# Input norm of a hybrid decoder layer: the refined reciprocal root kept in PSUM, its square taken by ScalarE

## The chip, the cores and the metric

One Trainium2 chip, one of its cores. The metric is the device time of one execution in microseconds; the kernel before has a median of 1319.98 us over 3 runs (1318.55 to 1320.32). The engines are named as the profile names them: PE (TensorE matmul), PEld (its weight loads), DVE (VectorE), ACT (ScalarE), POOL (GpSimd), SP (SyncE, which issues the DMAs).

## The reference

One layer over 1024 tokens of width 1024, all in float32. What matters here is the first step, an RMS norm whose result `u` feeds one wide projection; the two head groups, the output projection, a gated per-layer embedding and a final norm follow.

```python
def rmsnorm(x, w):
    xf = x.astype(jnp.float32)
    y = xf * lax.rsqrt(jnp.mean(xf * xf, axis=-1, keepdims=True) + NORM_EPS)
    return (y * w.astype(jnp.float32)).astype(x.dtype)

def reference(x, p, norm_w, w_in, ...):
    u = rmsnorm(h, norm_w[i])
    proj = jnp.einsum('bsd,de->bse', u, w_in[i])
    hq, hf, hi, hg, fq, fk, fv, fg, fz = jnp.split(proj, SPLIT_POINTS, axis=-1)
    y_h = hgrn2_branch(hq, hf, hi, lb_all[i], hgrn_gn[i]) * jax.nn.silu(hg)
    y_f = fox_branch(fq, fk, fv, fz, fox_fb[i]) * jax.nn.silu(fg)
    h = h + jnp.einsum('bse,ed->bsd', jnp.concatenate([y_h, y_f], axis=-1), w_out[i])
    ple = jnp.einsum('bsk,kd->bsd', p[i], w_ple[i])
    h = h + jax.nn.sigmoid(jnp.einsum('bsd,de->bse', h, w_ple_gate[i])) * ple
    return rmsnorm(h, final_norm_w)
```

## The kernel before

**Layout.** Activations lie transposed: 8 tiles of 128 channels (index k) by 1024 tokens. Tokens are worked in two halves of 512 (index c). Every float32 product is made of three matmuls on halves of a split: each operand is written as hi + lo, where hi is the value rounded by ACT to the matmul's input format (L82) and lo the rest, a subtraction on POOL or DVE (L83). L98, L99 and L100 are the three matmuls of a term.

**The opening, up to about 68 us.** x is loaded and squared (ACT), the squares of the 8 tiles are added up (DVE, `acc`), and one matmul with a matrix of ones (L253, L257) leaves in a PSUM bank `ssq[c]` the sum of squares of each token, the same in all 128 partitions. `rstd` (L119 to L122) makes the reciprocal root of it: ACT's table function gives y, and DVE refines it by one Newton step, y (1.5 - 0.5 s y y) with s the mean square. Then `u_norm` (L275) multiplies each of the 8 tiles of x by norm_w (a per-partition scalar) and by the root, in place, on DVE, and `u_split` makes uhi (ACT) and ulo (DVE for k = 0, 3, 7, POOL for the other five). Half 0 goes first, then half 1.

PE meanwhile makes `pple`, 16 pieces of p times w_ple, which ACT or DVE halves into `pleo` and SP stores for the end, and then `token_major`, the first 8 blocks of values v: blocks 0 to 3 need u of half 0, blocks 4 to 7 u of half 1, each of them 24 matmuls over all 8 tiles k. DVE copies each block out of PSUM (L149). POOL also makes the lo parts of the first weights (`wtlo`, then `wlo`).

**Order.** What is passed through `pin` keeps the order of the program on its engine; each engine runs its instructions in that order and waits at one for what it needs. So a DVE instruction that is late makes all DVE instructions behind it late. The matmuls of `token_major` are not pinned and are placed between the pinned ones by the scheduler.

**After the opening** come dense projections (L364), among which the recurrent heads and then the attention heads are worked in pieces, the output projection, the gate and the final norm. The final norm calls `rstd` too (L1094 on), which stays as it is.

**PSUM.** `pple` has 4 banks, `ssq` 2, and the products `ps` 2.

Of the kernel before, what the change touches and what calls it, by code (L numbers as in the profile page):

```python
# [12 lines left out]
AF = mybir.ActivationFunctionType  # L13
ALU = mybir.AluOpType
# [5 lines left out]
D = 1024  # L20
# [44 lines left out]
def trunk(ctx: ExitStack, tc: tile.TileContext, a, out):  # L65
    nc = tc.nc
# [18 lines left out]
    def load_w(src, k, lo_engine=None, pin=lambda ins: ins):  # L85

        wf = wpool.tile([P, KT, P], F32, name="wf", tag="wf", bufs=2)
        nc.sync.dma_start(out=wf[:, :k], in_=src)
        hi = wpool.tile([P, KT, P], F32R, name="whi", tag="whi")
        lo = wpool.tile([P, KT, P], F32R, name="wlo", tag="wlo")  # L90
        split(hi[:, :k], lo[:, :k], wf[:, :k], lo_engine or nc.gpsimd, pin)
        return hi, lo
# [24 lines left out]
    def rstd(y, t, ps, pin=lambda ins: ins):  # L117

        pin(nc.scalar.activation(y, ps, AF.Abs_reciprocal_sqrt, scale=1.0 / D))  # L119
        pin(nc.vector.tensor_tensor(out=t, in0=y, in1=y, op=ALU.mult))  # L120
        pin(nc.vector.scalar_tensor_tensor(out=t, in0=ps, scalar=-0.5 / D, in1=t, op0=ALU.mult, op1=ALU.mult))
        pin(nc.vector.scalar_tensor_tensor(out=y, in0=t, scalar=1.5, in1=y, op0=ALU.add, op1=ALU.mult))  # L122

    def operands(*names):

        return [[tuple(upool.tile([P, CH], F32R, name=name, tag="u") for name in names) for _ in range(KT)] for _ in range(NCH)]


    wt_st = ExitStack()
# [13 lines left out]
    def token_major(w, v, blocks, evac_pin=lambda ins: ins):  # L143

        for b in blocks:
            ps = pp.tile([P, 2 * P], F32, name="ps", tag="proj")
            sl = slice(b % 4 * P, (b % 4 + 1) * P)
            product(ps, [(u[b // 4][j][0][:, sl], u[b // 4][j][1][:, sl], w[0][:, j], w[1][:, j]) for j in range(KT)])
            evac_pin(nc.vector.tensor_copy(out=v[:, :, b], in_=ps.rearrange("p (i d) -> p i d", i=2)))  # L149

    with ExitStack() as st:
# [3 lines left out]
        pin = tc.keep_in_program_order  # L155

        vecs = const.tile([P, 4, KT], F32, name="vecs")
        norm_w, gn_w, lb_log, fin_w = (vecs[:, i, :] for i in range(4))
# [36 lines left out]
        def ple(*pieces):  # L195
            for i in pieces:
                n, c = i % KT, i // KT
                _, hi, lo = wple[n // 4]
                pple[i] = sps.tile([P, CH], F32, name="pple", bufs=4)
                product(  # L200
                    pple[i], [(hi[:, n % 4, j], lo[:, n % 4, j], phi[:, j, half[c]], plo[:, j, half[c]]) for j in range(2)], pin
                )

        def ple_out(i, act):
            n, c = i % KT, i // KT
            o = sp2.tile([P, CH], F32, name="pleo", bufs=7)
            if act:
                pin(nc.scalar.activation(o, pple[i], AF.Copy, scale=0.5))
            else:
                pin(nc.vector.tensor_scalar(out=o, in0=pple[i], scalar1=0.5, scalar2=None, op0=ALU.mult))  # L210
            nc.sync.dma_start(out=pled[n, :, half[c]], in_=o)
# [40 lines left out]
        ssq = [sps.tile([P, CH], F32, name="ssq") for _ in range(NCH)]  # L252
# [6 lines left out]
        first_pair = [wt.tile([P, KT, 2 * P], F32R, name=name) for name in ("wthi", "wtlo")]  # L259
        rs, newt = ([sp2.tile([P, CH], F32, name=name) for _ in range(NCH)] for name in ("rstd", "newt"))  # L260
        u = operands("uhi", "ulo")
        cst = const.tile([P, P + 32], F32, name="cst")
        nc.sync.dma_start(out=cst, in_=a["consts"])
# [4 lines left out]
        def split_pair(i):  # L268
            sl = slice(i * P, (i + 1) * P)
            split(first_pair[0][:, :, sl], first_pair[1][:, :, sl], wf_v[i], nc.gpsimd, pin)  # L270

        def u_norm(k, c):
            x = xs[k][:, half[c]]
            pin(
                nc.vector.scalar_tensor_tensor(  # L275
                    out=x, in0=x, scalar=norm_w[:, k : k + 1], in1=rs[c], op0=ALU.mult, op1=ALU.mult
                )
            )

        def u_split(k, c, lo_engine):  # L280
            split(*u[c][k], xs[k][:, half[c]], lo_engine, pin)

        v = v0p.tile([P, 2, FB, P], F32, name="v", tag="v")
        split_pair(0)
        rstd(rs[0], newt[0], ssq[0], pin)
        split_pair(1)
        ple_out(7, True)
        ple(11)
        for c in range(NCH):
            for k in range(KT):  # L290
                u_norm(k, c)
                if k:
                    u_split(k - 1, c, nc.vector if k - 1 in (0, 3, 7) else nc.gpsimd)
                if c and k in (0, 1, 4, 6):
                    b = (0, 1, 4, 6).index(k)
                    token_major(first_pair, v, range(b, b + 1), pin)
                if c == 0 and k in (2, 4, 6, 7):
                    i = 8 + (2, 4, 6, 7).index(k)
                    ple_out(i, True)
                    ple(i + 4)  # L300
            u_split(7, c, nc.vector)
            if c == 0:
                rstd(rs[1], newt[1], ssq[1], pin)
                for i in range(12, 16):
                    ple_out(i, True)
            else:
                first_f = load_w(a["w_in"][T_HF], KT, nc.gpsimd, pin)
                token_major(first_pair, v, range(FB // 2, FB))
# [192 lines left out]
    with ExitStack() as st:  # L501
# [8 lines left out]
        for i in range(2):  # L510
            t = hs.tile([P, FB, P], F32, name=f"st{i}")
            nc.gpsimd.memset(t, 0.0)
            st_t.append(t)
            t = hs.tile([P, FB, 32], F32, name=f"r{i}")
# [256 lines left out]
    with fox as st:  # L771
# [181 lines left out]
        for n, ch in enumerate(chunks):  # L953
            p, i, c = ch.p, ch.i, ch.c
# [33 lines left out]

        first_w = ahead.weights()
        y_h = operands("yhi", "ylo")  # L990
        for c in range(NCH):
            sl = slice(c * CH, (c + 1) * CH)
# [4 lines left out]
    with ExitStack() as st:  # L997
# [34 lines left out]
        with tc.tile_pool(name="yp", bufs=2 * KT, reuse_waits="tile") as yp:  # L1032

            y_f = [[] for _ in range(NCH)]
            w = [first_w, load_w(a["w_out"][1], KT, nc.vector, tc.keep_in_program_order)]
            for n in range(KT):
                dense(None, y_h, ev_h1(n), w=w[n])
                w.append(load_w(a["w_out"][n + 2], KT, nc.vector, tc.keep_in_program_order))
                hi, lo = (yp.tile([P, S], F32R, name=name, tag="y") for name in ("yhi", "ylo"))
                y = g01.tile([P, S], F32, name="yf", tag="g")  # L1040
                nc.sync.dma_start(out=y, in_=yd[KT + n])
                split(hi, lo, y, nc.vector, tc.keep_in_program_order)
                for c in range(NCH):
                    y_f[c].append(tuple(t[:, c * CH : (c + 1) * CH] for t in (hi, lo)))
            for n in range(2):
                gw[n] = load_gate(n, g01, ("ghi", "glo"), tag="g")

            hm = operands("hh", "hl")
            for n in range(KT):
                dense(a["w_out"][KT + n], y_f, ev_h(n), lo_engine=nc.vector, w=w[KT + n] if n < 2 else None)  # L1050
# [109 lines left out]
```

## Time and profile before

| | |
|---|---|
| median of 3 runs | 1319.98 us (1318.55 to 1320.32) |
| the profiled execution | 1317.97 us |
| its span, first to last instruction | 1316.2 us |
| mean granted PE clock | 0.994 |
| busy: PE, DVE, ACT, POOL | 1270.2, 799.8, 475.0, 351.2 us |
| first dense product (L364) | at 68.11 us |

A row of the timeline reads: start in us, duration in us, engine, line, operation, output <- inputs, shape, count; in brackets the idle time of the engine before it and what ended that. A row with x2 or x3 stands for so many instructions in a line, and its duration runs from the first start to the last end. The duration of an instruction holds whatever it waits for once it has been started. A group row gives the shortest, the median and the longest duration in ns, or the busy time and the mean. A windows row gives, for a stretch, each engine's busy time with the number of instructions, the granted clock, the DMA share and GB/s.

### The profile page before, as it was taken

The page shows a single profiled execution, that of the slowest core. Times are in us where ns is not written, and L with a number is a line of the kernel's source. Part 1 is how long each engine was busy: PE and PEld are TensorE (multiplying, and loading weights), DVE is VectorE, ACT ScalarE, POOL GpSimd, SP SyncE. Part 2 cuts the span into 40 slices and gives each one's busy share as a digit, 9 for nine tenths or more (in the row PEclk, how much of TensorE's full clock was granted, in tenths as well). Part 3 has the DMA queues.
Part 4 walks back from the last instruction along what each step waited for, and adds up shares of the span by engine and source line. Part 5 has one row for each costly group of instructions (what it writes and reads, how often), then busy time and mean ns, then how long its engine had stood idle before and what let it go on. Part 6 is the DMA issues. An engine that isn't in the chain of part 4 may idle for free.

```text
span 1316.2 us, 26795 instructions
## 1 busy us (share of the span) xinstructions
PE 1270.2 (97%) x10996; PEld 1014.5 (77%) x10996; DVE 799.8 (61%) x1988; ACT 475.0 (36%) x1144; POOL 351.2 (27%) x288
## 2 busy tenths in 40 slices
PE   6899999999999999999999999999999999999996
PEld 4787888889788877776777777776666788888895
DVE  6746565745657486377666666667788733333465
ACT  5523121312313124254444444444554411212454
POOL 3613122111212122324342434332322200102232
PEclk9999999999999999999999999999999999999998
DMA  7312102111111020211221212121232653212321
GB/s 290 131 48 65 50 18 80 49 34 48 50 49 33 33 64 22 81 58 57 90 72 59 74 58 74 57 74 57 81 101 79 211 194 99 80 48 74 118 79 66
DMA packets 38970, 102.22 MB, mean 78 GB/s; under 512 B 6720, under 2 KB 8896, under 8 KB 38848
## 3 DMA queue, kind: packets, MB, share of 16 engines
q1 hardware_dynamic: 38704, 99.99, 22.9%
q8 instruction: 86, 1.41, 0.4%
q0 software_dynamic: 144, 0.52, 0.1%
q14 instruction: 36, 0.29, 0.1%
HBM read 83.07 MB, written 17.43 MB: 76 GB/s over the span
## 4 chain that ended last, share of the span: by engine, by line
PE 80%; DVE 9%; ACT 6%; issue 2%; DMA 1%; POOL 1%; SPq 0%; DVEq 0%; ACTq 0%; POOLq 0%
PE ps L364 46%; PE lg L816 5%; PE ps L100 4%; PE po L864 4%; PE ps L98 4%; PE ps L99 4%; ACT x L852 2%; PE ps L571 1%; PE gps L100 1%; PE gps L99 1%; PE gps L98 1%; DVE x L275 1%; PE po L712 1%; PE po L714 1%; DVE x L830 1%
## 5 line engine op out<-in xcount | busy, mean ns | idle before, releaser
L364 PE MATMUL ps<-uhi,whi 128*128 128x512 f32 x896 | 360.1, 402 | 0.0
L364 PE MATMUL ps<-ulo,whi 128*128 128x512 f32 x896 | 354.4, 396 | 0.0
L364 PE MATMUL ps<-uhi,wlo 128*128 128x512 f32 x896 | 352.5, 393 | 0.0
L83 POOL TENSOR_TENSOR wlo<-wf,whi 128x1024 fp32r<-128x1024 f32 x59 | 144.9, 2456 | 453.4 <-ACT whi L82 424.1
L364 PEld LDWEIGHTS ps<-uhi,whi 128*128 128x128 f32 x896 | 168.2, 188 | 58.5 <-issue 21.6
L364 PEld LDWEIGHTS ps<-uhi,wlo 128*128 128x128 f32 x896 | 168.4, 188 | 35.6 <-issue 1.1
L364 PEld LDWEIGHTS ps<-ulo,whi 128*128 128x128 f32 x896 | 168.4, 188 | 33.6 <-issue 0.7
L852 ACT ACTIVATE x<-x,mxo 128x512 f32<-128x512 f32 (+15 forms) x256 | 130.4, 511 | 68.4 <-DVE mxo L840 68.4
L82 ACT CAST whi<-wf 128x1024 fp32r<-128x1024 f32 (+1 forms) x77 | 79.7, 1036 | 204.2 <-PE ps L99 89.8
L830 DVE CUSTOM_DVE_ANT_0 x<-lg,fb 128x512 f32<-128x512 f32 (+15 forms) x256 | 101.8, 434 | 78.4 <-PE lg L816 71.5
L853 DVE STREAM_TRANSPOSE pt<-x 128x512 f32<-128x512 f32 (+15 forms) x256 | 115.1, 457 | 37.9 <-ACT x L852 33.9
L98 PE MATMUL ps<-yhi,whi 128*128 128x512 f32 x256 | 99.8, 390 | 1.7 <-DVE h L1012 1.7
L99 PE MATMUL ps<-ylo,whi 128*128 128x512 f32 x256 | 99.7, 390 | 0.3 <-DVE ylo L83 0.3
L100 PE MATMUL ps<-yhi,wlo 128*128 128x512 f32 x256 | 99.6, 389 | 0.0
L816 PE MATMUL lg<-k,q 64*32 64x480 f32 (+15 forms) x1024 | 74.4, 396 | 2.6 <-DVE mx L830 2.6
L816 PE MATMUL lg<-k,qx 64*32 64x512 f32 (+15 forms) x1024 | 74.4, 396 | 0.0
L864 PEld LDWEIGHTS po<-pt,v 64*64 64x64 f32 x1536 | 53.6, 133 | 22.7 <-issue 9.2
L864 PE MATMUL po<-pt,v 64*64 64x256 f32 (+7 forms) x1536 | 69.4, 320 | 0.0
L98 PEld LDWEIGHTS ps<-yhi,whi 128*128 128x128 f32 x256 | 48.0, 188 | 12.2 <-ACT whi L82 2.1
L99 PEld LDWEIGHTS ps<-ylo,whi 128*128 128x128 f32 x256 | 48.1, 188 | 10.7 <-DVE ylo L83 0.8
L100 PEld LDWEIGHTS ps<-yhi,wlo 128*128 128x128 f32 x256 | 48.0, 188 | 9.8
L364 PE MATMUL ps<-wthi,uhi 128*128 128x256 f32 x192 | 54.0, 281 | 0.0
(205 smaller groups left out, 2158.0 us busy)
## 6 DMA issues: line engine op xcount, KB each, us to landing
wf<-in_w_in_dram SPq DMA_DIRECT2D x64, 512.0 KB, 3.5
fb<-fd SPq DMA_DIRECT2D x64, 128.0 KB, 3.2
yf<-yd SPq DMA_DIRECT2D x16, 512.0 KB, 5.9
wf<-in_w_out_dram SPq DMA_DIRECT2D x16, 512.0 KB, 3.6
x<-in_xT_dram SPq DMA_DIRECT2D x8, 512.0 KB, 9.4
pled<-pleo SPq DMA_DIRECT2D x16, 256.0 KB, 3.3
yd<-sg SPq DMA_DIRECT2D x8, 512.0 KB, 2.6
rz<-zd SPq DMA_DIRECT2D x16, 256.0 KB, 3.4
```

Of the source, the lines that this page charges most:

```text
L82: pin(nc.scalar.copy(hi, src))
L83: pin(lo_engine.tensor_tensor(out=lo, in0=src, in1=hi, op=ALU.subtract))
L98: pin(mm(ps, whi, uhi, start=i == 0, stop=False))
L99: pin(mm(ps, whi, ulo, start=False, stop=False))
L100: pin(mm(ps, wlo, uhi, start=False, stop=i == n - 1))
L275: nc.vector.scalar_tensor_tensor(out=x, in0=x, scalar=norm_w[:, k : k + 1], in1=rs[c], op0=ALU.mult, op1=ALU.mult)
L364: pe(mm(ps, x, y, start=i == j == 0, stop=i == n - 1 and j == 2))
L816: mm(ps[32 * j : 32 * j + 32, m % 2, : 32 * n], q[:, 32 * (j // 2) :][:, :32], k[not own][rows].rearrange("p (t a k) -> p t a k", a=2, k=3 ...
L830: nc.vector.tensor_tensor_reduce(out=x, in0=ps[:, m % 2, : 32 * n], in1=copies[m % 2][:, : 32 * n], scale=1.0, scalar=BIG, op0=ALU.add, op ...
L852: nc.scalar.activation(x, x, AF.Exp, bias=self.other[:, g : g + 1], scale=-1.0, accum_out=zs[:, m : m + 1])
L853: nc.vector.transpose(self.probs[:, : m + 1, g], x.rearrange("p (t k) -> p t k", k=32))
L864: mm(po[half[t % 2], r, 32 * first : 256], v_t[self.p][half[r], t ^ r, half[self.i]], self.probs[half[r], t, first:].rearrange("p g q -> p ...
```

## The change

A new helper `rstd_in_place` stands in for `rstd` at the two calls of the input norm. ACT makes the first estimate y as before (now L130) and also its square (L131, into the tile `newt`). DVE then makes the Newton step in two instructions that write into the bank of `ssq` itself: L132 replaces s by -0.5 s y y, L133 that by (1.5 + it) y. `u_norm` (now L282) takes its factor from `ssq[c]` in PSUM and no longer from the SBUF tile `rs[c]`. The same numbers are multiplied in the same order; the square is made by another engine.

```diff
+    def rstd_in_place(y, t, ps, pin):
+        pin(nc.scalar.activation(y, ps, AF.Abs_reciprocal_sqrt, scale=1.0 / D))
+        pin(nc.scalar.activation(t, y, AF.Square))
+        pin(nc.vector.scalar_tensor_tensor(out=ps, in0=ps, scalar=-0.5 / D, in1=t, op0=ALU.mult, op1=ALU.mult))
+        pin(nc.vector.scalar_tensor_tensor(out=ps, in0=ps, scalar=1.5, in1=y, op0=ALU.add, op1=ALU.mult))
...
@@ u_norm
-                    out=x, in0=x, scalar=norm_w[:, k : k + 1], in1=rs[c], op0=ALU.mult, op1=ALU.mult
+                    out=x, in0=x, scalar=norm_w[:, k : k + 1], in1=ssq[c], op0=ALU.mult, op1=ALU.mult
...
-        rstd(rs[0], newt[0], ssq[0], pin)
+        rstd_in_place(rs[0], newt[0], ssq[0], pin)
...
-                rstd(rs[1], newt[1], ssq[1], pin)
+                rstd_in_place(rs[1], newt[1], ssq[1], pin)
```

All lines behind the helper are 7 higher in the changed kernel (L275 is L282, L149 is L156). On DVE, at the start of half 0, the order of instructions changes thus (`x_92` and `x_93` are the tiles of x for k = 0 and 1):

```order
 L115 TENSOR_TENSOR acc<-acc,sq 128x512 x2
-L120 TENSOR_TENSOR newt<-rstd 128x512
-L121 SCALAR_TENSOR_TENSOR newt<-ssq,newt 128x512
-L122 SCALAR_TENSOR_TENSOR rstd<-newt,rstd 128x512
-L275 SCALAR_TENSOR_TENSOR x_92<-x_92,vecs,rstd 128x512
-L275 SCALAR_TENSOR_TENSOR x_93<-x_93,vecs,rstd 128x512
+L132 SCALAR_TENSOR_TENSOR ssq<-ssq,newt 128x512
+L133 SCALAR_TENSOR_TENSOR ssq<-ssq,rstd 128x512
+L282 SCALAR_TENSOR_TENSOR x_92<-x_92,vecs,ssq 128x512
+L282 SCALAR_TENSOR_TENSOR x_93<-x_93,vecs,ssq 128x512
 L83 TENSOR_TENSOR ulo<-x_92,uhi 128x512
```

One instruction of three is gone, and the factor of the norm is read from `ssq`. The same holds at the start of half 1; behind it DVE's order is unchanged. On ACT, at the same place:

```order
 L82 CAST wthi<-wf 128x8x128
-L119 ACTIVATE rstd<-ssq 128x512
+L130 ACTIVATE rstd<-ssq 128x512
+L131 ACTIVATE newt<-rstd 128x512
 L82 CAST wthi<-wf 128x8x128
```

The square stands right behind the root, ahead of the second cast of the first weights. On PE three matmuls of `token_major` stand some places earlier, and POOL and SP have the same instructions in the same order.

## The prediction

> **What bounds the kernel now.** I read the share of the chain first, then three stretches of the span, then the rows of each engine between 25 and 60 us, where the changed lines run.
>
> ```profile
> PE 80%; DVE 9%; ACT 6%; issue 2%; DMA 1%; POOL 1%; SPq 0%; DVEq 0%; ACTq 0%; POOLq 0%
> ...
> 30.00:68.11 38.11, 32.06 (x220) 28.64 (x219) 29.37 (x33) 17.55 (x28) 24.43 (x17) 0.96 0.36 119
> 68.11:100.00 31.89, 31.89 (x143) 26.42 (x142) 14.51 (x28) 6.71 (x10) 4.78 (x2) 1.00 0.12 42
> 100.00:1316.20 1216.20, 1185.31 (x10565) 944.40 (x10563) 736.85 (x1910) 431.46 (x1081) 312.20 (x261) 0.99 0.22 71
> ...
> 68.11 0.39 PE L364 MATMUL ps<-uhi,whi 128*128 128x512 f32 x1
> ```
>
> The columns after the width are the busy time of PE, PEld, DVE, ACT and POOL, then the granted clock. From the first dense product at 68.11 us on, PE is busy 31.89 of 31.89 us and then 97%: what moves that start moves the end. Before it, PE is not the limit; DVE is, and half of its time there is waiting:
>
> ```profile
> 26.44 2.47 DVE L120 TENSOR_TENSOR newt<-rstd 128x512 f32<-128x512 f32 x1 [1.25 <-ACT rstd L119]
> 28.94 0.69 DVE L121 SCALAR_TENSOR_TENSOR newt<-ssq,newt 128x512 f32<-128x512 f32 x1
> 29.67 2.07 DVE L122 SCALAR_TENSOR_TENSOR rstd<-newt,rstd 128x512 f32<-128x512 f32 x1
> 31.78 1.42 DVE L275 SCALAR_TENSOR_TENSOR x<-x,vecs,rstd 128x512 f32<-128x512 f32 x2
> 33.21 0.69 DVE L83 TENSOR_TENSOR ulo<-x,uhi 128x512 fp32r<-128x512 f32 x1
> 33.82 4.12 DVE L275 SCALAR_TENSOR_TENSOR x<-x,vecs,rstd 128x512 f32<-128x512 f32 x3
> ...
> 43.29 1.02 DVE L83 TENSOR_TENSOR ulo<-x,uhi 128x512 fp32r<-128x512 f32 x1 [0.69 <-ACT uhi L82]
> ...
> 46.40 0.75 DVE L275 SCALAR_TENSOR_TENSOR x<-x,vecs,rstd 128x512 f32<-128x512 f32 x1
> ...
> 58.66 1.00 DVE L83 TENSOR_TENSOR ulo<-x,uhi 128x512 fp32r<-128x512 f32 x1 [0.68 <-ACT uhi L82]
> ...
> 25.96 5.24 POOL L83 TENSOR_TENSOR wtlo<-wf,wthi 128x1024 fp32r<-128x1024 f32 x2 [6.31 <-ACT wthi L82]
> ...
> L83 POOL TENSOR_TENSOR wtlo<-wf,wthi x2: 2402/2638/2875, 26.0 to 28.3; 128x1024 fp32r<-128x1024 f32 x2
> L83 POOL TENSOR_TENSOR ulo<-x,uhi x10: 1271/1722/1782, 33.9 to 57.4; 128x512 fp32r<-128x512 f32 x10
> L275 DVE SCALAR_TENSOR_TENSOR x<-x,vecs,rstd x16: 739/752/1781, 31.8 to 56.3; 128x512 f32<-128x512 f32 x16
> ```
>
> Two L275 side by side take 1.42 us, three 4.12. L120 ends (28.91) 0.55 us after POOL's first wtlo (25.96 + 2.40 = 28.36). POOL's second, begun at 28.33, then takes 2.875, 0.47 more than the first, and L122 ends (31.74) 0.54 us after it. So DVE and POOL take turns, whole instructions at a time. L121, between them, took 0.69 with POOL working: of its tensors ssq lies in PSUM. Later rows say the same more sharply:
>
> ```profile
> 137.00 2.94 POOL L83 TENSOR_TENSOR wlo<-wf,whi 128x1024 fp32r<-128x1024 f32 x1 [14.98 <-ACT whi L82]
> ...
> 137.61 2.88 DVE L579 TENSOR_TENSOR x<-x,f 128x512 f32<-128x512 f32 x1
> ...
> 531.82 2.39 POOL L83 TENSOR_TENSOR wlo<-wf,whi 128x1024 fp32r<-128x1024 f32 x1 [8.99 <-ACT whi L82]
> ...
> 532.27 0.69 DVE L441 SCALAR_TENSOR_TENSOR sg<-sg,ps 128x512 f32<-128x512 f32 x1 [3.17 <-ACT sg L440]
> ```
>
> L579 (both inputs in SBUF) is held 2.88 us beside a POOL subtraction; L441 (in1 in PSUM) runs in 0.69 inside one.
>
> **The change, part by part.** Each half of the sequence loses L120 on DVE and gains a Square on ACT. L132, L133 and the sixteen L282 have one SBUF tensor each instead of two, so by the rows above they no longer take turns with POOL. The six ulo subtractions that DVE does (k = 0, 3, 7) still do. Prices:
>
> ```profile
> 25.81 0.60 ACT L119 ACTIVATE rstd<-ssq 128x512 f32<-128x512 f32 x1
> 26.31 1.04 ACT L82 CAST wthi<-wf 128x1024 fp32r<-128x1024 f32 x1
> ...
> 43.65 2.05 ACT L208 ACTIVATE pleo<-pple 128x512 f32<-128x512 f32 x4
> ...
> L220 ACT ACTIVATE sq<-x x2: 621/626/632, 22.2 to 23.8; 128x512 f32<-128x512 f32 x2
> L82 ACT CAST uhi<-x 128x512 fp32r<-128x512 f32 x16 | 9.9, 621 | 16.4 <-DVE x L275 16.3
> L208 ACT ACTIVATE pleo<-pple 128x512 f32<-128x512 f32 x9 | 5.0, 598 | 0.0
> L741 DVE SCALAR_TENSOR_TENSOR sg<-pt,vecs,sg x16: 741/745/751, 142.9 to 528.4; 128x512 f32<-128x512 f32 x16
> L441 DVE SCALAR_TENSOR_TENSOR sg<-sg,ps x16: 649/685/689, 526.9 to 1033.0; 128x512 f32<-128x512 f32 x16
> ```
>
> Square 0.62 (L220, same size). L132 and L133 0.69 each (L121, L441). L282 0.745, the next starting 0.66 after (L741 has its operands: one PSUM, one SBUF, a pointer scalar). A handover costs 0.03 (26.41 to 26.44). I work the chain forward from 25.81, where nothing is changed yet.
>
> First root: 26.41, Square to 27.06, L132 to 27.78, L133 to 28.50, first x at 28.53 instead of 31.78. The Square pushes POOL's second wtlo by nothing: the cast that it waits for (1.04) now ends at 28.03, still before the first wtlo does (28.36).
>
> First half: two x to 29.94. ulo(0) meets POOL's second wtlo (28.33 to 30.73) and ends 0.54 later, 31.27. Three x to 33.25. ulo(3) meets POOL's ulo(2) (uhi(2) is there at 32.60, so 32.62 to 33.90) and ends at 34.45. Three x to 36.43. POOL's ulo(4), (5), (6), 1.28 each, end at 38.35; ulo(7) waits for them and ends at 38.90, instead of 44.31.
>
> Second root: ACT comes to it after uhi(7), at 37.77; Square to 39.02, L132 and L133 to 40.46, first x at 40.49 instead of 46.40. Behind this Square stand four pleo (2.05 us together, to 41.0) and then uhi(0), whose x is there at 41.24, so the Square is covered by 0.2 us; without that cover it would cost its 0.6.
>
> Second half: two x, two copies of v and ulo(0) to 43.18; three x to 45.16; ulo(3) behind POOL's ulo(2) (44.5 to 45.8) to 46.35; three x and two copies to 49.02; POOL's ulo(5) and (6) to 50.60; ulo(7) at 51.15 instead of 59.66. That is 8.5 us. The same working with the operations of before gives 43.9, 46.7 and 59.0 for the three points that were 44.3, 46.4 and 59.7; its own error is 0.6, so I take the difference of like with like, 59.0 - 51.15 = 7.9.
>
> PE next:
>
> ```profile
> 52.97 0.28 PE L100 MATMUL ps<-wthi,ulo 128*128 128x256 f32 x1
> ...
> 59.16 0.39 PE L100 MATMUL ps<-wthi,ulo 128*128 128x256 f32 x1 [1.06 <-POOL ulo L83]
> ...
> 60.13 0.42 DVE L149 COPY v<-ps 128x256 f32<-128x256 f32 x1 [0.48 <-PE ps L100]
> ...
> 59.05 0.95 POOL L512 MEMSET st<- 128x1024 f32 x1
> ...
> 30.39 0.39 PE L100 MATMUL pple<-phi,wlo 128*128 128x512 f32 x1
> ...
> 30.00:32.00 2.00, 0.78 (x4) 0.32 (x2) 1.97 (x2) 0.00 (x0) 1.20 (x1) 1.00 0.00 0
> 32.00:34.00 2.00, 0.66 (x4) 0.46 (x4) 1.98 (x4) 1.39 (x3) 0.08 (x1) 1.00 0.00 0
> 34.00:36.00 2.00, 2.00 (x7) 1.71 (x8) 2.00 (x2) 0.96 (x2) 2.00 (x2) 0.56 0.55 147
> 36.00:38.00 2.00, 2.00 (x10) 1.71 (x9) 2.00 (x3) 1.14 (x3) 1.40 (x1) 0.58 0.65 232
> L571 PE MATMUL ps<-x,k x1536: 206/206/230, 100.9 to 497.1; 128*32 128x48 f32 x192
> ```
>
> Blocks 0 to 3 of the first v ended at 53.25, 8.9 us after the first half's last ulo, and PE then waited for POOL and DVE. Now they end near 38.9 + 8.9 = 47.8. Block 4 ended as its copy of v began, at 60.13, and blocks 5 to 7 took the 8.0 us to 68.11: 2.7 for a block of 72/3 = 24 matmuls, 0.11 each. So PE could have block 4 done at 50.5, 0.6 before the last ulo (51.15). Before ulo(7) of the first half it has block 0 and four pieces of p times w_ple, 24 matmuls of 512 columns: 24 x 0.11 + 24 x 0.22 = 8 us, now in the 9.0 from 29.9 to 38.9 and with waits between. That may make it 0.7 late, of which the 0.6 covers most; I take 0.3 off. Blocks 5 to 7 follow as before.
>
> What is late next: the weights of the first dense product. POOL makes their wlo after ulo(6) and a memset, 50.6 + 0.95 + 2.40 = 54, needed at 60.5: hidden. The PSUM banks of ssq are held until the last L282 at 49.0; the pools that get them are first written at 100.9 (L571), now about 93. Both edits cost nothing there.
>
> Sum: 7.9 - 0.3 = 7.6 us. The profiled execution took 1317.97 (span 1316.2, 1.8 around it), so 1310.4. The median shown is 2.0 above that execution, so I predict 1319.98 - 7.6 = 1312.4.
>
> Unknown costs. DVE writes no PSUM in this trace: L132 and L133 lie at four places on the path. Nearest rows: 0.65 (L441's shortest) to twice 0.69, so -0.2 to +2.8 in all; I take 0.69, since reading from PSUM cost nothing over SBUF. PE's granted clock fell to 0.56 from 34 to 38 after 2.5 us without work (30.78 to about 33.2). That gap now nearly closes (first uhi 29.93, the last piece before it ends at 30.78); if the fall comes all the same, some 1.8 us more, of which 0.6 is covered.
>
> [...]
>
> **The rivals.** *The pointer scalar counts.* L282 keeps norm_w as a per-partition scalar in SBUF. If DVE fetches it as a second SBUF input, all sixteen stay in turn with POOL and only the roots gain. Working it so, the last ulo ends at 57.6 and the gain is 1.4: 1318.6. No row decides: L741 has such a scalar, but no POOL work ran beside any of its 16 (POOL is idle for 14.98 us up to 137.00 and done at 139.94; the first L741 starts at 142.9). [...]
>
> *PE takes over as the bound.* If PE runs 2.5 us late at block 0 (the clock's fall plus the packed pieces), block 4 ends 1.9 later: gain 6.0, 1314. For it: the 8 us of work in the 9 before ulo(7). Against it: no idle gap over 1.1 us is left there. At most, with the second half's ulo all in time, PE gives 38.9 + 8.9 + 2.7 + 8.0 = 58.5, a gain of 9.6.
>
> *Absorbed.* The dense products start earlier, but wait for weights later: 1320. Against it: from 68.11 to 100 PE never waits, and the loads of weights follow POOL and PE.
>
> *Slower.* Reading and writing one PSUM bank in the same instruction could run in turns. With all twenty operations at 1.3 us instead of 0.69 to 0.745 the gain is gone; at 1.5 the kernel is 4 us slower, 1324. For it: no row has DVE write PSUM. Against it: only four of the twenty do, and even at twice the time these cost 2.8.
>
> **How the numbers follow.** Forecast 0.68, PE takes over 0.14, pointer scalar 0.09, absorbed 0.05, slower 0.04. The first two make 0.82 and reach from the ceiling of 9.6 (1310.4) to 6.0 with half the PSUM writes' upper bound on top (1315.4); with a median's scatter of 0.9 the range is 1310.4 to 1316.2. A change under 0.2% (2.6 us) cannot be told from none: faster 0.82, same 0.14 (pointer scalar and absorbed), slower 0.04.
>
> **What would show it.** Right: no L282 above 0.8 us, L132 and L133 near 0.69, the first x at 28.5, the last DVE ulo at 51 to 52, the first dense product at 60 to 61, and the same stretch of PE after it. L282 at 1.7 beside POOL means the pointer scalar; PE without waits before block 4, or a granted clock of 0.56, means PE; a dense start at 60 with an end unmoved means absorbed.

## The result, and the profile after

The changed kernel takes 1310.61 us (median of 4 runs, 1309.77 to 1311.11) beside 1319.26 us for the kernel before (4 runs): a ratio of 0.9934 [0.9922, 0.9947], a gain of 8.65 us. A second set, with 5 runs of the changed kernel and 21 of the one before, gives 1310.07 (1309.78 to 1310.49) to 1319.0, 0.9932 [0.9918, 0.9945]. The prediction was 1312.4 with a range from 1310.4 to 1316.2, so the time lies in the range, near its lower end, and the gain is a microsecond larger than the 7.6 predicted.

The profiled execution of the changed kernel took 1311.11 us, its span is 1309.4. First, the chain that ended last, by engine, and the start of the dense products in PE's timeline:

```profile
PE 82%; DVE 7%; ACT 6%; DMA 2%; issue 2%; POOL 1%; SPq 0%; DVEq 0%; ACTq 0%; POOLq 0%
```

```profile
60.23 0.28 PE L100 MATMUL ps<-wthi,ulo 128*128 128x256 f32 x1
60.35 0.39 PE L371 MATMUL ps<-uhi,whi 128*128 128x512 f32 x1
```

DVE's share of the chain fell from 9% to 7%. The first dense product (L371, before L364) starts at 60.35 instead of 68.11, and from there to the end of the span it is 1249.05 us, before 1248.09. As a whole the stretch behind that start is 1.0 us longer in this execution, and in the second profile of the change, below, it is 1248.0, as before. The gain lies ahead of that start. DVE's timeline of that stretch (start, duration):

```profile
27.29 0.70 DVE L132 SCALAR_TENSOR_TENSOR ssq<-ssq,newt 128x512 f32<-128x512 f32 x1 [1.91 <-ACT newt L131]
28.02 0.70 DVE L133 SCALAR_TENSOR_TENSOR ssq<-ssq,rstd 128x512 f32<-128x512 f32 x1
28.76 1.41 DVE L282 SCALAR_TENSOR_TENSOR x<-x,vecs,ssq 128x512 f32<-128x512 f32 x2
30.19 1.31 DVE L83 TENSOR_TENSOR ulo<-x,uhi 128x512 fp32r<-128x512 f32 x1
31.42 2.05 DVE L282 SCALAR_TENSOR_TENSOR x<-x,vecs,ssq 128x512 f32<-128x512 f32 x3
...
38.09 1.13 DVE L83 TENSOR_TENSOR ulo<-x,uhi 128x512 fp32r<-128x512 f32 x1 [1.38 <-ACT uhi L82]
39.26 0.70 DVE L132 SCALAR_TENSOR_TENSOR ssq<-ssq,newt 128x512 f32<-128x512 f32 x1
39.99 0.70 DVE L133 SCALAR_TENSOR_TENSOR ssq<-ssq,rstd 128x512 f32<-128x512 f32 x1
40.72 0.75 DVE L282 SCALAR_TENSOR_TENSOR x<-x,vecs,ssq 128x512 f32<-128x512 f32 x1
...
50.53 1.06 DVE L83 TENSOR_TENSOR ulo<-x,uhi 128x512 fp32r<-128x512 f32 x1 [0.69 <-ACT uhi L82]
52.07 0.42 DVE L156 COPY v<-ps 128x256 f32<-128x256 f32 x1 [0.48 <-PE ps L100]
```

Three L282 in a line now take 2.05 us; the three L275 of the kernel before took 4.12. The subtractions that DVE does itself (L83, both inputs in SBUF) are still held: 1.31, 1.13, 1.06 instead of about 0.69. The views by tile and by line give shortest, median and longest duration in ns; POOL's subtractions had a median of 1722 before:

```profile
L83 POOL TENSOR_TENSOR ulo<-x,uhi x10: 1291/1302/1732, 30.9 to 49.7; 128x512 fp32r<-128x512 f32 x10
L83 DVE TENSOR_TENSOR ulo<-x,uhi x6: 683/1176/1308, 30.2 to 50.5; 128x512 fp32r<-128x512 f32 x6
```

```profile
L282 DVE SCALAR_TENSOR_TENSOR x<-x,vecs,ssq x16: 731/736/750, 28.8 to 49.1; 128x512 f32<-128x512 f32 x16
```

All sixteen L282, most of them beside POOL's work, are between 731 and 750 ns. The gain is on both engines, as turn-taking holds both: POOL's median subtraction is 0.42 us shorter.

Last, three stretches of the windows view (width, then busy time of PE, PEld, DVE, ACT, POOL, then the granted clock, DMA share, GB/s), to be read against the rows of the prediction for the same stretches:

```profile
30.00:32.00 2.00, 1.96 (x11) 1.38 (x10) 1.97 (x3) 1.28 (x3) 2.00 (x2) 1.00 0.12 45
34.00:36.00 2.00, 1.78 (x10) 1.56 (x10) 2.00 (x4) 1.05 (x3) 1.52 (x2) 1.00 1.01 321
36.00:38.00 2.00, 2.00 (x14) 1.76 (x13) 0.71 (x2) 2.00 (x6) 1.88 (x2) 1.00 0.86 325
```

PE has no gap around 32 us any more, and the granted clock stays at 1.00 where it was 0.56 and 0.58.

### The profile page after: what moved, and what is told of

Read it like the earlier page. It is cut to its first block, busy times and chain, and to the rows that moved or that the text cites. A ratio compares the mean times of both kernels' runs of the same rounds, so it can differ in the third digit from the quotient of the medians.

```text
span 1309.4 us, 26795 instructions
## 1 busy us (share of the span) xinstructions
PE 1268.6 (97%) x10996; PEld 1014.2 (77%) x10996; DVE 787.7 (60%) x1986; ACT 475.9 (36%) x1146; POOL 348.8 (27%) x288
## 4 chain that ended last, share of the span: by engine, by line
PE 82%; DVE 7%; ACT 6%; DMA 2%; issue 2%; POOL 1%; SPq 0%; DVEq 0%; ACTq 0%; POOLq 0%
PE ps L371 47%; PE ps L100 5%; PE lg L823 5%; PE ps L98 5%; PE ps L99 5%; PE po L871 4%; ACT x L859 2%; PE ps L578 1%; PE gps L99 1%; PE gps L98 1%; PE gps L100 1%; PE po L721 1%; PE po L719 1%; DVE x L837 1%; DMA wf<-in_w_in_dram 1%
## 5 line engine op out<-in xcount | busy, mean ns | idle before, releaser
L371 PE MATMUL ps<-uhi,whi 128*128 128x512 f32 x896 | 360.0, 402 | 0.0
L371 PE MATMUL ps<-ulo,whi 128*128 128x512 f32 x896 | 354.3, 395 | 0.0
L371 PE MATMUL ps<-uhi,wlo 128*128 128x512 f32 x896 | 352.6, 393 | 0.0
L83 POOL TENSOR_TENSOR wlo<-wf,whi 128x1024 fp32r<-128x1024 f32 x59 | 145.3, 2462 | 452.8 <-ACT whi L82 423.4
L371 PEld LDWEIGHTS ps<-uhi,whi 128*128 128x128 f32 x896 | 168.2, 188 | 58.5 <-issue 21.6
L371 PEld LDWEIGHTS ps<-uhi,wlo 128*128 128x128 f32 x896 | 168.4, 188 | 35.6 <-issue 1.1
L371 PEld LDWEIGHTS ps<-ulo,whi 128*128 128x128 f32 x896 | 168.4, 188 | 33.5 <-issue 0.7
L371 PE MATMUL ps<-wthi,uhi 128*128 128x256 f32 x192 | 54.0, 281 | 0.0
```

Source lines behind the costliest of these rows:

```text
L83: pin(lo_engine.tensor_tensor(out=lo, in0=src, in1=hi, op=ALU.subtract))
L371: pe(mm(ps, x, y, start=i == j == 0, stop=i == n - 1 and j == 2))
```

## The experiments

My theory: what the change gains is turns. A DVE instruction with two tensors in SBUF and a POOL subtraction exclude each other for whole instructions, and the change takes twenty DVE instructions out of that. The rivals were that it is the shorter root (an instruction less on DVE), that PE sets the start of the dense products, and that it is the number of DVE instructions that counts. Each run is read by its median and by the time from ACT's first root to the first dense product, since the root itself starts some tenths earlier or later from one execution to the next.

| kernel | median us (runs) | before us (runs) | ratio | first root | first dense product | between |
|---|---|---|---|---|---|---|
| before | | | | 25.81 | 68.11 | 42.30 |
| the change again | 1310.07 (5) | 1319.0 (21) | 0.9932 [0.9918, 0.9945] | 26.12 | 60.20 | 34.08 |
| square on ACT alone | 1318.11 (11) | 1319.0 (21) | 0.9992 [0.9983, 1.0] | 26.16 | 67.17 | 41.01 |
| the new root alone | 1317.52 (11) | 1319.0 (21) | 0.9989 [0.9981, 0.9998] | 25.74 | 66.34 | 40.60 |
| the factor in PSUM alone | 1313.32 (5) | 1319.0 (21) | 0.9957 [0.9944, 0.9969] | 25.92 | 63.50 | 37.58 |
| all ulo on DVE, else as before | 1313.39 (5) | 1318.42 (9) | 0.9958 [0.9945, 0.997] | 25.60 | 63.20 | 37.60 |
| the change, PE lighter | 1309.41 (5) | 1318.42 (9) | 0.9931 [0.9918, 0.9943] | 26.18 | 60.19 | 34.01 |
| the change, running sum in PSUM too | 1308.28 (5) | 1318.42 (9) | 0.9921 [0.9907, 0.9934] | 24.81 | 58.82 | 34.01 |

### The change again

The same kernel, run beside its parts.

> The change itself once more, beside the others: 8 us below before, first dense product at 60.4. In the first profile the blocks of v took 2.83 us each on PE, against 2.72 in the profile of before; if that belongs to the change it is there again, if it is the one execution it is not.

It took 8.9 us less than the kernel before. Its last ulo ends at 51.75 and the dense products start 8.45 us later, as in the kernel before (59.66 to 68.11). In the first profile of the change it was 8.76: there each block of v took 2.83 us, here 2.72 as before. So the 2.83 does not belong to the change, which has both. It is there again in the profiles of two other runs below, all ulo on DVE and the lighter PE, each time with a granted clock of 1.00; what sets it stays open.

### Square on ACT alone

```diff
-        pin(nc.vector.tensor_tensor(out=t, in0=y, in1=y, op=ALU.mult))
+        pin(nc.scalar.activation(t, y, AF.Square))
```

This is done in a copy of `rstd` that the two calls of the input norm use. The other two steps and the factor stay in SBUF.

> One part alone: the square of the estimate on ScalarE, the refinement and the factor in SBUF as in the kernel before. Theory of turns (a DVE instruction with two SBUF tensors and POOL's subtractions shut each other out, whole instructions at a time; one with a PSUM tensor does not): the second refinement step and all sixteen u_norm still take turns with POOL, so the Square saves only the wait of L120; first dense product 1.1 us earlier (67.0), time 1.1 us below before. Rival, the shorter root: the gain comes from the DVE instruction that is gone, twice; the first dense product would be 4 us or more earlier.

Measured 0.9 us, [0, 2.2] by the interval. DVE's timeline, and POOL's two subtractions in it:

```profile
27.46 0.69 DVE L128 SCALAR_TENSOR_TENSOR newt<-ssq,newt 128x512 f32<-128x512 f32 x1 [1.92 <-ACT newt L127]
28.18 1.08 DVE L129 SCALAR_TENSOR_TENSOR rstd<-newt,rstd 128x512 f32<-128x512 f32 x1
29.30 3.45 DVE L282 SCALAR_TENSOR_TENSOR x<-x,vecs,rstd 128x512 f32<-128x512 f32 x2
...
26.30 5.24 POOL L83 TENSOR_TENSOR wtlo<-wf,wthi 128x1024 fp32r<-128x1024 f32 x2 [6.30 <-ACT wthi L82]
```

The first x starts 2.5 us earlier than before (29.30, 31.78), but now meets POOL's second wtlo, which ends at 31.54, and the pair takes 3.45 instead of 1.42. It ends at 32.75, before at 33.20. The stall was not removed, it moved to the next instruction with two SBUF tensors.

### The new root alone

```diff
-        pin(nc.vector.scalar_tensor_tensor(out=ps, in0=ps, scalar=1.5, in1=y, op0=ALU.add, op1=ALU.mult))
+        pin(nc.vector.scalar_tensor_tensor(out=y, in0=ps, scalar=1.5, in1=y, op0=ALU.add, op1=ALU.mult))
@@ u_norm
-                    ... in1=ssq[c] ...
+                    ... in1=rs[c] ...
```

Against the change: the refined root goes back to SBUF and the norm reads it there.

> The change without its last part: Square on ScalarE, first refinement step in PSUM, but the second writes the root to the SBUF tile rs, and u_norm reads it there. Theory of turns: the roots no longer wait for POOL, but all sixteen u_norm do, 1.7 us where POOL works; first dense product 1.4 us earlier (66.7), time 1.4 us below before. Rival, the shorter root: nearly all of the change's 8.7 us.

Measured 1.5 us. DVE's timeline again:

```profile
27.77 0.69 DVE L133 SCALAR_TENSOR_TENSOR rstd<-ssq,rstd 128x512 f32<-128x512 f32 x1
28.50 3.40 DVE L282 SCALAR_TENSOR_TENSOR x<-x,vecs,rstd 128x512 f32<-128x512 f32 x2
...
32.53 4.12 DVE L282 SCALAR_TENSOR_TENSOR x<-x,vecs,rstd 128x512 f32<-128x512 f32 x3
```

The root is as fast as in the change (first x at 28.50), and most of it is lost again in the very next pair, 3.40 us. So the shorter root is not the cause of the gain.

### The factor in PSUM alone

```diff
+    def rstd_out(y, t, ps, pin):
+        pin(nc.scalar.activation(y, ps, AF.Abs_reciprocal_sqrt, scale=1.0 / D))
+        pin(nc.vector.tensor_tensor(out=t, in0=y, in1=y, op=ALU.mult))
+        pin(nc.vector.scalar_tensor_tensor(out=t, in0=ps, scalar=-0.5 / D, in1=t, op0=ALU.mult, op1=ALU.mult))
+        pin(nc.vector.scalar_tensor_tensor(out=ps, in0=t, scalar=1.5, in1=y, op0=ALU.add, op1=ALU.mult))
@@ u_norm
-                    ... in1=rs[c] ...
+                    ... in1=ssq[c] ...
...
-        rstd(rs[0], newt[0], ssq[0], pin)
+        rstd_out(rs[0], newt[0], ssq[0], pin)
...
```

Against the kernel before. The root's three steps on DVE as before, but the last writes the PSUM bank, and the norm reads it there.

> The last part alone: the root is made as in the kernel before, all three steps on DVE from SBUF, only its last instruction writes to PSUM, and u_norm reads its factor there. Theory of turns: the root still waits for POOL (2.5 and 2.1 us), no u_norm does (0.75 each); first dense product 4.9 us earlier (63.2), time 4.9 us below before. Rival, the shorter root: within 1 us of before.

Measured 5.7 us. DVE's timeline:

```profile
26.55 2.47 DVE L127 TENSOR_TENSOR newt<-rstd 128x512 f32<-128x512 f32 x1 [1.25 <-ACT rstd L126]
...
29.78 2.08 DVE L129 SCALAR_TENSOR_TENSOR ssq<-newt,rstd 128x512 f32<-128x512 f32 x1
31.89 1.41 DVE L282 SCALAR_TENSOR_TENSOR x<-x,vecs,ssq 128x512 f32<-128x512 f32 x2
...
33.94 2.06 DVE L282 SCALAR_TENSOR_TENSOR x<-x,vecs,ssq 128x512 f32<-128x512 f32 x3
```

The root is held as before (L127 2.47, L129 2.08), and the norm is free (2.06 for three). From root to dense product the two parts gain 1.70 and 4.72, together 6.42; the whole change gains 8.22. The other 1.8 are had only together: the time that the root saves lasts only if what follows it is not held in its place. The first x starts 5.97 us after ACT's root here, as before, and 2.76 after it in the new root alone, where 2.0 of these 3.2 are lost again in the next pair. PE, whose granted clock fell to 0.50 for a while in this run (last section), has little part in the 1.8: the dense products start 8.45 us behind the last ulo here too, and DVE waits for PE only 0.40 us more than in the change.

### All ulo on DVE, else as before

```diff
-                    u_split(k - 1, c, nc.vector if k - 1 in (0, 3, 7) else nc.gpsimd)
+                    u_split(k - 1, c, nc.vector)
```

The other way to end the turns: POOL has nothing but one memset to do between 31.0 and 56.2 us. DVE gets ten instructions more, with root and factor in SBUF as before. If DVE's count of instructions were what matters, this would be slower.

> The kernel before, root and factor in SBUF as they were; only the ten ulo subtractions that POOL made in the opening are made by DVE too, which gives DVE ten instructions more. Theory of turns: with POOL silent between 31 and 60 us every u_norm takes 0.75 us and every ulo 0.69, so the last ulo is done earlier in spite of ten more instructions: first dense product about 3 us earlier (65), time 3 us below before. Rival, the count of DVE instructions: ten more at 0.61 us apart, 6 us later (74), time 6 us above before.

Measured 5.0 us faster. Groups of DVE between 24 and 64 us (busy, mean ns), the last row that of the kernel before:

```profile
L275 DVE SCALAR_TENSOR_TENSOR x<-x,vecs,rstd 128x512 f32<-128x512 f32 x16 | 11.9, 748 | 0.1
L83 DVE TENSOR_TENSOR ulo<-x,uhi 128x512 fp32r<-128x512 f32 x16 | 11.0, 688 | 0.2
...
L275 DVE SCALAR_TENSOR_TENSOR x<-x,vecs,rstd 128x512 f32<-128x512 f32 x16 | 17.9, 1160 | 0.1
```

The same L275 that average 1160 ns in the kernel before take 748 as soon as POOL is silent, with both tensors in SBUF. The gain was larger than I expected (about 3): the last ulo ends at 55.90, 3.8 us earlier than before, and the dense products start 7.30 behind it and not 8.45. What I had left out is that PE gets the ulo at an even pace here and has part of block 5 done when the last one comes. From 46 to 60 us it never stops; the second row is the kernel before:

```profile
46.00:60.00 14.00, 14.00 (x121) 14.00 (x120) 10.67 (x19) 7.48 (x10) 3.79 (x5) 1.00 0.18 51
...
46.00:60.00 14.00, 10.95 (x86) 9.89 (x85) 12.91 (x16) 6.35 (x10) 8.56 (x7) 1.00 0.29 96
```

In that stretch of the kernel before PE was busy 10.95 us of 14. So in this kernel PE's own work leaves no room, and its 5.0 us are no measure of all that the turns cost. PE's granted clock also fell here, to 0.53 and 0.62 from 34 to 38 us (last section); how much of the gain that took is not measured.

### The change, PE lighter

```diff
+                if i >= 12:
+                    for j in range(2):
+                        pin(mm(pple[i], hi[:, n % 4, j], phi[:, j, half[c]], start=j == 0, stop=j == 1))
+                    continue
```

Of the pieces 12 to 15 of p times w_ple only the product of the hi halves is made: sixteen matmuls less, some 3.5 us of PE at 0.22 each, an estimate from the 31.89 us for 143 matmuls behind the dense start before. The four matmuls with a lo part are left out of each of these pieces. In the change PE is busy 30.07 of the 30.35 us up to the dense start, so it could have been the bound.

> The change, with the four pieces of p times w_ple of the first half of u (pieces 12 to 15) made of two matmuls each instead of six: the lo terms of these pieces are left out, so that PE has 16 matmuls of 512 columns, 3.6 us, less to do between 31 and 39 us. If PE has taken over as the bound of the opening: first dense product up to 3 us earlier (57.3 to 59). If the turns of POOL and DVE that are left (ulo of k = 0, 3, 7) still set the end: block 3 is done earlier, the last ulo is not, and the first dense product moves by 0.4 us or less (60.0 at the earliest).

The dense products start at 60.19 instead of 60.20. The last three blocks of v took 2.83 us each in this profile and 2.72 in the other, so at the same pace they would have started about 0.3 earlier, still within the 0.4 expected. PE's waits between 30 and 61 us (total, times, longest):

```profile
PE ps L98 <- DVE v L156: 1.8, 1, 1.8
PE ps L100 <- POOL ulo L83: 1.1, 3, 0.6
```

In the change run beside its parts it waited 0.2 in that stretch. What PE no longer had to do became waiting, 2.9 us. So DVE and POOL set the start in the change, and a lighter PE alone gains next to nothing. The two are nearly even, though: with only 0.2 us of waits left on PE, a DVE that is faster in this stretch alone could, by that count, gain little more than that; no run tried it.

### The change, running sum of squares in PSUM too

```diff
+        ssq = [sps.tile([P, CH], F32, name="ssq") for _ in range(NCH)]
...
-                pin(nc.scalar.activation(acc, xs[k], AF.Square))
+                for c in range(NCH):
+                    pin(nc.scalar.activation(ssq[c], xs[k][:, half[c]], AF.Square))
...
-                add_squares(acc[:, sl], sq[:, sl], k == 1, pin)
+                for c in range(NCH):
+                    if k < KT - 1:
+                        add_squares(ssq[c], sq[:, half[c]], k == 1, pin)
+                    elif sl == half[c]:
+                        pin(nc.vector.tensor_tensor(out=acc[:, sl], in0=ssq[c], in1=sq[:, sl], op=ALU.add))
...
```

The same thought a stage earlier: while the squares are added up, POOL subtracts too. The running sum is kept in the two `ssq` banks, in halves; the last addition writes the SBUF tile that the matmul with ones reads.

> The change, and the same remedy one step earlier: the running sum of the squares is kept in the two PSUM banks that later take the matmul's sums, in halves of 512 columns, so that the adds of k = 1 to 6 have one SBUF tensor each; the last adds write the sum to SBUF for the matmul as before. It computes the same. In the profiles so far two adds took 3.57 us and two 4.14 us beside POOL's subtractions, against 2.46 unhindered. Theory of turns: the adds take 0.69 a half throughout, the reciprocal root on ScalarE starts 1 to 2 us earlier (24.0 to 25.0), and first dense product and time follow by 1 to 1.5 us against the change; what is not gained is lost to more instructions and to the loads of x. Rival, the opening is paced by the loads of x up to there: no gain, or 0.6 us worse by the seven instructions more.

Additions of four halves (two tiles) in DVE's timeline:

```profile
14.24 2.69 DVE L115 TENSOR_TENSOR ssq<-ssq,sq 128x512 f32<-128x512 f32 x4 [0.68 <-ACT sq L229]
...
18.25 2.72 DVE L115 TENSOR_TENSOR ssq<-ssq,sq 128x512 f32<-128x512 f32 x4 [0.73 <-ACT sq L229]
```

In the kernels before and after the same two tiles take (here of the change):

```profile
14.02 3.57 DVE L115 TENSOR_TENSOR acc<-acc,sq 128x1024 f32<-128x1024 f32 x2 [0.74 <-ACT sq L227]
...
18.10 4.14 DVE L115 TENSOR_TENSOR acc<-acc,sq 128x1024 f32<-128x1024 f32 x2
```

2.3 us less on DVE; as it now waits for squares, 1.3 of it arrive at the first root (24.81 instead of 26.12), and from there it is the change again, 34.01 to 34.08. The median is 1308.28 (1308.06 to 1308.44), 10.1 us faster than the kernel before and the best of these. Against the change, which ran in another set, it gains 1.8 us by the medians, 1.2 by the distance of each from the kernel before in its own set, and 1.38 by the dense start.

## Why the prediction was right, point by point

- **Turn-taking** was the term that carried the sum, and it stands. It was taken away in two ways that have nothing else in common, a factor in PSUM (5.7 us) and a silent POOL (5.0 us), and both times the norm's instructions went to 0.74 to 0.75. L275, with x and the root in SBUF, has a mean of 1160 ns before, and L282, in the same groups view, 738.
- **The pointer scalar** does not count as a second input: L282, with norm_w in SBUF, was never above 750 ns. This rival would have had it near 1.7 (L275's longest before was 1781 ns).
- **Prices.** L132 and L133 take 0.70 at all four places (0.69 taken), so reading and writing the same PSUM bank costs 0.01 more, 0.04 in all, and neither the +2.8 of the bound nor the slower rival came. L282 has a median of 0.736 (0.745 taken).
- **PSUM as a source** cost nothing over SBUF here, as the prediction read it from L441 (685 ns) and L83 (0.69 us): L282 takes 738 ns with its factor in PSUM, L275 748 with it in SBUF beside a silent POOL.
- **The four points of time.** First x 28.76 (28.53 predicted), ulo(7) of half 0 at 39.22 (38.90), second x 40.72 (40.49), last ulo 51.59 (51.15). The first root started 0.18 later than in the trace the working began from; without that the misses are 0.05, 0.14, 0.05 and 0.26. The last ulo moved by 8.07 us, and 7.9 were predicted; that they are so close is in part chance, by the later root.
- **Like with like** is a term that was mis-sized. The working forward gave 8.5 us for the last ulo, and 0.6 was taken off as the working's own error. Counted from ACT's first root, the last ulo ends after 33.85 us before and after 25.60 and 25.63 in the two profiles of the change: 8.25 and 8.22. More than half of what was taken off should have stayed.
- **The Square on ACT** was covered at the second root as said: the four pleo behind it end at 41.16, and uhi(0) waits until 41.51 for its x. The cover is 0.35 (0.2 predicted).
- **PE** is the other term that was mis-sized. I took 0.3 off for a late block 4; nothing was to be taken off. The half clock did not come (1.00 from 30 us to the dense start), and in the second profile of the change the dense products start 8.45 us after the last ulo, exactly as before. That makes the shift of the dense start 7.8 and 7.9 in the two profiles, not 7.6. PE without waits before block 4 was to be the sign that PE takes over, and PE's waits for ulo there were down to 0.2 us in all. The lighter PE shows that it was not the bound, but also how near it is.
- **Weights and PSUM banks** hid as said: POOL's wlo ends at 54.3 (54 predicted), and the stretch behind the dense start is 1.0 us longer than before in one profile and as long in the other, so at most that was absorbed.
- **The rest of the difference**, from 7.8 or 7.9 in the traces to 8.65 and 8.9 in the medians, is within what the interval leaves open (7.0 to 10.3 us for the first set). I don't assign it to a cause.
- **The time and the range.** The 1312.4 was counted from 1319.98, the median of three runs; with the fourth run the kernel before has 1319.26. Of the miss of 1.8 us, 1.05 lie in the gain and 0.7 in this. The range had a median's scatter added at its upper end and none at its lower, which was the most that PE allowed. 1310.61 lies 0.2 us inside that end and the 1310.07 of the second set 0.3 outside, so that the time fell into the range is partly luck.

## What to carry to other kernels

When a DVE row shows two durations for one shape, the long one ending about half a microsecond after a POOL subtraction (0.55 and 0.54 us here), look at how many of its tensors lie in SBUF: here one operand in a PSUM bank that was there anyway took the instruction out of the turns, at the same price within 0.01 us, and POOL's median subtraction became 0.42 us shorter as well. Free the run of instructions behind it too, because a root alone that was freed lost 2.0 of its 3.2 us to the next pair. Then look for the next bound: here PE has 0.2 us of waits left, so by that count a still faster DVE would soon meet it, while an earlier start of the whole stretch still moved the dense products, by 1.4 us.

## What the runs showed of the hardware that I had not expected

**Ten instructions more on the busiest engine of a stretch made the kernel 5.0 us faster.** In the kernel before, DVE was busy 12.91 of the 14 us from 46 to 60, but much of its busy time was waiting (its sixteen L275 took 17.9 us in the opening, and 11.9 beside a silent POOL); the work that POOL took from it there cost it more than it saved.

**PE's clock fell after a wait of 2.5 us and not after one of 1.7.** PE waits at about 31 us for the first uhi. PE's waits between 20 and 69 us, of the factor alone and then of the square alone:

```profile
PE ps L98 <- ACT uhi L82: 2.5, 1, 2.5
```

```profile
PE ps L98 <- ACT uhi L82: 1.7, 1, 1.7
```

The windows of the same two kernels a little later:

```profile
34.00:36.00 2.00, 1.97 (x8) 1.73 (x8) 2.00 (x4) 1.70 (x4) 1.87 (x2) 0.50 0.38 128
36.00:38.00 2.00, 2.00 (x10) 1.69 (x9) 1.98 (x3) 1.05 (x3) 1.63 (x2) 0.71 0.82 250
```

```profile
34.00:36.00 2.00, 1.98 (x12) 1.50 (x10) 2.00 (x3) 0.76 (x2) 2.00 (x2) 1.00 0.68 178
36.00:38.00 2.00, 0.99 (x5) 0.91 (x6) 2.00 (x2) 1.44 (x3) 0.95 (x1) 1.00 0.68 244
```

The wait is 2.5 us in the kernel before too, and with all ulo on DVE, which has 0.53 and 0.62 there; it is 1.2 us with the root alone and none in the change, and both have 1.00. Five kernels and the one before sort themselves by the length of that wait: 2.5 us in the three whose clock fell, 1.7 or less in the others. They sort in the same way by how little PE does around it: from 30 to 34 us it is busy 1.42 to 1.54 us in the three whose clock fell and 2.12 or more in the others. No run varied the one without the other, so which of them counts is not shown.
